# Second stream's low-rank intermediates in their own buffers, and four kinds of scratch stores issued from GpSimd's queue

## The chip, the cores and the metric

The kernel runs on one core of a Trainium2 chip. The engines are TensorE (PE in the profile, with its weight loads listed as PEld), VectorE (DVE), ScalarE (ACT), GpSimd (POOL) and SyncE (SP). SP computes nothing here: its queue issues most of the DMA transfers; GpSimd's queue issues others. Each engine works through its own instructions in order and waits on semaphores for the others. The metric is the device time of one execution in microseconds (us), the median of several runs.

## The reference

A two-layer encoder is applied to two independent requests (here: stream 0 and stream 1), each 512 tokens by 1024 features, in float32, with shared weights.

```python
def _trunk(x, pre_norm_g, post_norm_g, rwkv_params, na_params):
    for i in range(DEPTH):                       # DEPTH = 2
        xn = _rms_norm(x, pre_norm_g[i])
        h = _rwkv7_branch(xn, ...) if i == 0 else _natten_branch(xn, ...)
        x = x + _rms_norm(h, post_norm_g[i])
    return x
# in _rwkv7_branch; lerp(j) = xn + (0.5 * (x_prev + x_next) - xn) * mu[j]
r, k, v, z = lerp(0) @ w_r, lerp(1) @ w_k, lerp(2) @ w_v, xn @ w_z
for d in range(2):                               # forward and backward
    w_log = -softplus(-(w0[d] + tanh(lerp(3 + d) @ w1[d]) @ w2[d])) - 0.5
    decay = exp(-exp(w_log))
    a = sigmoid(a0[d] + (lerp(5 + d) @ a1[d]) @ a2[d])
    y += scan(r, decay, k * (1 + (a - 1) * k_a), v, -kk, kk * a)  # kk: k, scaled and normalised
out = (group_norm(y) + bonus) * silu(z) @ w_o
```

The part that the change touches first is the low-rank pair `tanh(x @ w1) @ w2` and `(x @ a1) @ a2`: 1024 features go down to 64 and up again to 1024, for each of the two directions. The 64-wide intermediates are four arrays per stream (q = 0 to 3). The second layer is a gated attention over a neighbourhood in a 8 by 64 grid.

## The kernel before, in words

Feature rows lie on the 128 partitions and the 512 tokens along the free dimension, so a 1024-feature array is eight tiles of 128x512. Every large product is done as three float32r products of high and low halves (`halves`, L379 and L380; in the scan L743 and L745), accumulated in PSUM.

The program has three stages.

**The prelude** (`prelude`, first for stream 0, then for stream 1) normalises the input, makes the token-shifted mixtures and computes the low-rank intermediates. For each pair of them (`q2` = 0, 1) it forms a 128x512 sum `y` in a buffer `lr` (L582 to L589), and ScalarE writes each 64-row half of it through Tanh or a copy to `u` (L591). `u` is the other half of the same buffer `lr`, so both halves of a pair use one place, and there is one `lr` in all. For stream 0, `u` goes straight to `hidden`, which splits it for later use. For stream 1 it is stored to scratch in HBM (`save("hid", ...)`, L595, which issues in L327) and loaded again when stream 1's turn in the scan comes (L863). Two more buffers of the prelude matter below: `lm`, a 128x514 array with its two edge columns set to zero by GpSimd (L576, L577), and `ls`, four rotating 128x512 buffers that the mixtures pass through on their way to HBM.

**The scan** (`scan_phase`) runs the recurrence in chunks of 64 tokens, 64 steps in all, for both streams. Its instructions are ordered for TensorE, VectorE and ScalarE by a planner (`weave` with the class `Clock`): threads emit steps, and a model of each engine's time chooses which thread goes next. Threads beside the recurrence are: `preps`, which turns k, r and the low-rank arrays into the scan's operands (`prep`: loads `rb` and `k`, then L876; `w2` is split by L878 and L880; L894 and L895 multiply the split weight by the intermediates); `inverse`; `finish`, which normalises a finished output and stores it as `y` (L1316); and `flow`, which feeds big matrix products (L824 to L826) into TensorE's free time, among them the output projection of stream 0, whose result `h` is stored (L1336), and the residual sum `x1` (L781, stored in L782). Where nothing is ready, the planner puts in short idle-filling matmuls (L1641). SP's and GpSimd's own orders follow from the order in which the program emits and from the scheduler's estimates.

**The rest** (`rest`) does the second layer's attention and projections for both streams, with products in L430 to L432.

Scratch loads are always issued from SP (`load`, L333). Scratch stores go through `save` (L325 to L327), whose queue `store` chooses: before the scan SP; from the scan's beginning (`away` is set) GpSimd, except for the kinds `y`, `x1` and `h`, which stay on SP. A store or load waits in its queue until its source is written, or its destination is free, and everything behind it in that queue waits as well.

Names in the profile are those of the program: a DMA `dhid<-lr` is the store of a low-rank intermediate, `dy<-sz` of `y`, `dh<-tmp` of `h`, `dx<-xr` and `dx<-act` of `x1`; `raw` are weights on their way to `whi` and `wlo`.

Of the kernel before, what the change touches and what calls it, by code (L numbers as in the profile page):

```python
# [11 lines left out]
F32 = mybir.dt.float32  # L12
# [7 lines left out]
P = 128  # L20
T = 512
# [210 lines left out]
class Trunk:  # L232
# [94 lines left out]
        self.store(kind).dma_start(d, src)  # L327

    def store(self, kind):
        return self.nc.gpsimd if self.away and kind not in ("y", "x1", "h") else self.nc.sync  # L330

    def load(self, dst, src):
        self.nc.sync.dma_start(dst, src)  # L333
# [168 lines left out]
    def prelude(self, s):  # L502
        nc = self.nc
        vt, gps, act = nc.vector, nc.gpsimd, nc.scalar
        xs = []
        if s == 0:
            self.vectors()
        for k in range(KT):
            if s == 0 and k == self.WFIRST:
                self.first = [self.weight(self.a["w_z"][0])]  # L510
            t = self.t("xn", (P, T + 2), 16, F32, self.lp)
            self.load(t[:, 1:T + 1], self.a["x"][s][k * P:(k + 1) * P, :])
            xs.append(t)
            if s == 0:

                lo, hi = self.pair()
                act.activation(hi, t[:, 1:T + 1], AF.Identity, scale=self.vec("pre0", k))
                vt.scalar_tensor_tensor(lo, t[:, 1:T + 1], self.vec("pre0", k), hi.bitcast(F32), op0=ALU.mult, op1=ALU.subtract)
                self.xz.append((hi, lo))
                yield  # L520
        if s == 0:
            self.consts()
        acc = self.t("acc") if s else self.t("vs", bufs=self.NVS)
        for k, t in enumerate(xs):
            gps.memset(t[:, 0:1], 0.0)
            gps.memset(t[:, T + 1:T + 2], 0.0)
            self.sumsq(acc, t[:, 1:T + 1], k, vt if s or k % 2 else vt)
            yield
        rstd = self.rstd(acc)
        if s == 0:  # L530
            self.rstd0 = rstd
        yield
        xn, xx = [], []
        for k, t in enumerate(xs):
            x = t[:, 1:T + 1]
            vt.scalar_tensor_tensor(x, x, self.vec("pre0", k), rstd, op0=ALU.mult, op1=ALU.mult)
            xn.append(x)
            yield
        if s == 0:
            yield from self.lora_weights()  # L540
        for k, t in enumerate(xs):
            u = self.t("xx", (P, T), 16, F32, self.lp)
            vt.tensor_tensor(u, t[:, 2:T + 2], t[:, 0:T], op=ALU.add)
            xx.append(u)
            yield
        self.shift[s] = xn, xx

        def mixed(kind, j, k):

            t = self.t("ls", (P, T), 4, F32, self.lp)  # L550
            self.lerp(t, xn[k], xx[k], 8 * j + k)
            self.save("l" + kind, s, k, t)

        pm = self.p("pf", (P, 2, T))
        ps = (self.p("pm"), self.p("us"))
        for k in range(KT):
            if s == 0:
                hi, lo = self.xz[k]
            else:
                hi, lo = (self.t("ls", (P, T), 4, F32R, self.lp) for _ in range(2))  # L560
                self.halves(xn[k], lo, hi, self.alt(k))
            for q2 in range(2):
                for out, w in ((pm[:, q2], self.wm), (ps[q2], self.wl)):
                    a, b = (m[:, k % 4] for m in w[2 * q2 + k // 4])
                    nc.tensor.matmul(out, a, hi, start=(k == 0), stop=False)
                    nc.tensor.matmul(out, a, lo, start=False, stop=False)
                    nc.tensor.matmul(out, b, hi, start=False, stop=(k == KT - 1))
                yield
            for kind, j in (("k", 1), ("r", 0), ("v", 2)) if s else ():
                mixed(kind, j, k)  # L570
                yield
        for q2 in range(2):
            mw = self.t("lm", (P, KT * P), 1, F32, self.lp)[:, 0:T + 2]
            lr = self.t("lr", (P, KT * P), 1, F32, self.lp)
            y, u = lr[:, 0:T], lr[0:64, T:2 * T]
            gps.memset(mw[:, 0:1], 0.0)  # L576
            gps.memset(mw[:, T + 1:T + 2], 0.0)  # L577
            if s == 0:
                vt.tensor_tensor(mw[:, 1:T + 1], pm[:, q2], rstd, op=ALU.mult)
            else:  # L580
                act.copy(mw[:, 1:T + 1], pm[:, q2])
            vt.tensor_tensor(y, mw[:, 2:T + 2], mw[:, 0:T], op=ALU.add)  # L582
            yield
            vt.scalar_tensor_tensor(mw[:, 1:T + 1], y, 0.5, mw[:, 1:T + 1], op0=ALU.mult, op1=ALU.subtract)
            if s == 0:
                vt.tensor_tensor(y, ps[q2], rstd, op=ALU.mult)
                vt.tensor_tensor(y, y, mw[:, 1:T + 1], op=ALU.add)
            else:
                vt.tensor_tensor(y, ps[q2], mw[:, 1:T + 1], op=ALU.add)  # L589
            for q in (2 * q2, 2 * q2 + 1):  # L590
                act.activation(u, y[64 * (q % 2):64 * (q % 2) + 64], AF.Tanh if q < 2 else AF.Copy)  # L591
                if s == 0:
                    self.hidden(q, u)
                else:
                    self.save("hid", s, q, u)  # L595
            yield
        if s == 0:
            for k in range(KT):
                mixed("v", 2, k)
                yield  # L600
        if s == 1:
            for k in range(KT):
                self.save("lz", s, k, xn[k])
# [1326 lines left out]
```

## Time and profile before

| | us |
|---|---|
| median of 3 runs (lowest, highest) | 1659.32 (1658.92, 1660.64) |
| the profiled execution's own time | 1659.26 |
| its span, first to last instruction | 1657.5 |
| TensorE busy in it | 1557.6 (94%) |
| VectorE busy | 1217.3 (73%) |
| ScalarE busy | 1013.8 (61%) |
| GpSimd busy | 175.8 (11%) |
| mean granted TensorE clock | 0.975 of full speed |

The profiled execution's time is its span and 1.8 us around it, and it stands at the median of the runs. Times in the text are counted from the start of the span. In the order of time the prelude ends at about 185 us, the scan at about 1165 us. In a timeline row the columns are start, duration, engine, line, operation, `out<-in` with partitions by elements, the count of merged instructions, and in brackets how long the engine stood idle just before and what ended that. Busy time does not count the issuing of DMAs.

### The profile page before, as it was taken

To read this page: it belongs to the slowest core of one execution; us is meant where nothing else is said; L and a number is where in the kernel's file an instruction comes from. 1 tells how busy PE (TensorE), PEld (TensorE's weight loads), DVE (VectorE), ACT (ScalarE), POOL (GpSimd) and SP (SyncE) were. 2 spreads that over 40 slices of the span, in tenths; PEclk is the share of its full clock that TensorE was granted. 3 is DMA by queue.
4 is the path that set the end of the run, shared out by engine and by line. 5 is a ranking of instruction groups with operands and counts; after the bars stand their busy time and mean duration, and the time that the engine had idled before them with its cause. 6 is when DMAs were issued, how large, how long until landed. Compare 5 with 4: busy or idle time off the path is not lost.

```text
span 1657.5 us, 46539 instructions
## 1 busy us (share of the span) xinstructions
PE 1557.6 (94%) x18826; PEld 1197.0 (72%) x18826; DVE 1217.3 (73%) x2711; ACT 1013.8 (61%) x2027; POOL 175.8 (11%) x334
## 2 busy tenths in 40 slices
PE   7989798898999998998988999999999999999998
PEld 6867566776667776776666777777777788777776
DVE  8886469688789787897788897855577585665564
ACT  6567565766755677665575665454567665455562
POOL 0000113311101223010000011000000002100000
PEclk9989899999999999999987999999999999999999
DMA  6455578676687687675776675553765346745553
GB/s 212 154 177 180 163 247 282 211 248 214 228 263 238 209 264 249 207 252 171 243 233 227 201 251 168 178 188 126 265 224 174 109 140 205 246 158 175 171 164 103
DMA packets 176312, 336.29 MB, mean 203 GB/s; under 512 B 20928, under 2 KB 53824, under 8 KB 176096
## 3 DMA queue, kind: packets, MB, share of 16 engines
q1 hardware_dynamic: 152800, 253.60, 48.0%
q0 software_dynamic: 23296, 79.71, 13.6%
q8 instruction: 148, 2.42, 0.6%
q14 instruction: 68, 0.56, 0.1%
HBM read 227.71 MB, written 105.51 MB: 201 GB/s over the span
## 4 chain that ended last, share of the span: by engine, by line
PE 47%; DVE 8%; ACT 5%; DMA 4%; issue 3%; SPq 0%; POOL 0%; DVEq 0%; ACTq 0%; POOLq 0%
PE pg L430 6%; PE pg L431 6%; PE pg L432 6%; PE pm L824 4%; PE pm L825 3%; PE pm L826 3%; PE pf L1112 2%; PE sc L1450 2%; PE po L1483 2%; PE pt L1468 2%; PE us L1231 1%; PE zy L1184 1%; PE us L1211 1%; PE zy L1235 1%; DMA raw<-in_w_in_dram 1%
## 5 line engine op out<-in xcount | busy, mean ns | idle before, releaser
L824 PE MATMUL pm<-act,whi 128*128 128x512 f32 x640 | 285.0, 445 | 8.1 <-ACT act L793 3.2
L825 PE MATMUL pm<-act,whi 128*128 128x512 f32 x640 | 258.0, 403 | 11.7 <-DVE act L771 6.5
L826 PE MATMUL pm<-act,wlo 128*128 128x512 f32 x640 | 256.4, 401 | 5.3 <-DVE wlo L745 5.3
L824 PEld LDWEIGHTS pm<-act,whi 128*128 128x128 f32 x640 | 122.8, 192 | 51.1 <-issue 10.8
L430 PE MATMUL pg<-act,whi 128*128 128x512 f32 x384 | 158.6, 413 | 0.4 <-DVE tmp L1406 0.4
L379 ACT CAST whi<-raw 128x512 fp32r<-128x512 f32 x148 | 91.3, 617 | 106.5 <-PE pg L431 68.7
L431 PE MATMUL pg<-act,whi 128*128 128x512 f32 x384 | 152.6, 397 | 0.0
L432 PE MATMUL pg<-act,wlo 128*128 128x512 f32 x384 | 152.6, 397 | 0.0
L825 PEld LDWEIGHTS pm<-act,whi 128*128 128x128 f32 x640 | 123.5, 193 | 37.9 <-DVE act L771 16.8
L826 PEld LDWEIGHTS pm<-act,wlo 128*128 128x128 f32 x640 | 123.2, 192 | 35.0 <-DVE wlo L745 8.2
L380 DVE TENSOR_TENSOR wlo<-raw,whi 128x512 fp32r<-128x512 f32 x148 | 101.4, 687 | 60.9 <-ACT whi L379 60.2
L745 DVE TENSOR_TENSOR wlo<-raw,whi 128x512 fp32r<-128x512 f32 x160 | 109.1, 684 | 36.4 <-ACT whi L743 36.2
L743 ACT CAST whi<-raw 128x512 fp32r<-128x512 f32 x160 | 97.8, 617 | 42.0 <-PE pm L825 24.3
L430 PEld LDWEIGHTS pg<-act,whi 128*128 128x128 f32 x384 | 72.3, 188 | 15.6 <-issue 3.3
L432 PEld LDWEIGHTS pg<-act,wlo 128*128 128x128 f32 x384 | 72.2, 188 | 14.8 <-issue 0.3
L431 PEld LDWEIGHTS pg<-act,whi 128*128 128x128 f32 x384 | 72.5, 189 | 14.0 <-issue 2.5
L1016 DVE TENSOR_TENSOR etmp<-N 128x30 f32<-128x30 f32 (+14 forms) x240 | 78.6, 328 | 4.3
L1018 DVE TENSOR_TENSOR N<-etmp,N 128x30 f32<-128x30 f32 (+14 forms) x240 | 78.7, 328 | 4.0
L1461 DVE CUSTOM_DVE_ANT_0 sb<-sc,bias 128x256 f32<-128x256 f32 x128 | 49.2, 419 | 27.7 <-PE pt L1468 21.5
L1464 ACT ACTIVATE sb<-sb,mx 128x256 f32<-128x256 f32 x128 | 64.0, 502 | 6.9 <-DVE mx L1463 6.7
L1112 PE MATMUL pf<-cab 64*64 64x128 f32 (+1 forms) x2048 | 66.8, 267 | 0.5 <-issue 0.5
L1135 DVE TENSOR_TENSOR AK<-zy,cc 128x256 f32<-128x256 f32 x63 | 26.6, 422 | 52.0 <-PE zy L1090 51.9
(407 smaller groups left out, 3680.5 us busy)
## 6 DMA issues: line engine op xcount, KB each, us to landing
dab<-ab POOLq DMA_DIRECT2D x32, 1024.0 KB, 7.1
cab<-dab SPq DMA_DIRECT2D x64, 512.0 KB, 4.6
raw<-in_w_in_dram SPq DMA_DIRECT2D x128, 256.0 KB, 3.0
bias<-in_rpb_dram SPq DMA_DIRECT2D x32, 384.0 KB, 5.2
raw<-in_w_z_dram SPq DMA_DIRECT2D x32, 256.0 KB, 3.2
raw<-in_w_k_dram SPq DMA_DIRECT2D x32, 256.0 KB, 3.7
raw<-in_w_r_dram SPq DMA_DIRECT2D x32, 256.0 KB, 3.6
k<-dk SPq DMA_DIRECT2D x32, 256.0 KB, 3.6
```

The source lines that it names most:

```text
L379: self.nc.scalar.copy(hi, src)
L380: (eng or self.nc.vector).tensor_tensor(lo, src, hi.bitcast(F32), op=ALU.subtract)
L430: nc.tensor.matmul(ps, hi, x[k][0], start=(k == 0), stop=False)
L431: nc.tensor.matmul(ps, hi, x[k][1], start=False, stop=False)
L432: self.mm = nc.tensor.matmul(ps, lo, x[k][0], start=False, stop=(k == KT - 1))
L743: nc.scalar.copy(hi, raw[h])
L745: nc.vector.tensor_tensor(lo, raw.pop(h), hi.bitcast(F32), op=ALU.subtract)
L824: nc.tensor.matmul(ps, hi[:, at], xh, start=(k == 0), stop=False)
L825: nc.tensor.matmul(ps, hi[:, at], xl, start=False, stop=False)
L826: nc.tensor.matmul(ps, lo[:, at], xh, start=False, stop=(k == KT - 1))
L1018: vt.tensor_tensor(N[:, q + 1:, :q], tv, N[:, q + 1:, :q], op=ALU.add)
L1112: end = nc.tensor.matmul(st.f[half(a), h, 0, d, g] if st.last else st.f[half(a), h, :, d, g], ab[half(h), d, g, 2 * e[d] + 1 - a], rt if s ...
```

## The change

Two lines decide it. The store's queue is now GpSimd for `hid` always and for every kind once the scan has begun, so that 4 stores of `hid` before the scan and 16 of `y`, 8 of `h` and 8 of `x1` in it move from SP's queue to GpSimd's. And stream 1's four intermediates are written to buffers of the rotating `ls` set, of which there are four, instead of to the second half of `lr`.

```diff
     def store(self, kind):
-        return self.nc.gpsimd if self.away and kind not in ("y", "x1", "h") else self.nc.sync
+        return self.nc.gpsimd if kind == "hid" or self.away else self.nc.sync
...
             for q in (2 * q2, 2 * q2 + 1):
+                if s:
+                    u = self.t("ls", (P, T), 4, F32, self.lp)[0:64]
                 act.activation(u, y[64 * (q % 2):64 * (q % 2) + 64], AF.Tanh if q < 2 else AF.Copy)
                 if s == 0:
                     self.hidden(q, u)
                 else:
                     self.save("hid", s, q, u)
```

No arithmetic is added or removed. Two lines are inserted, so that line numbers from 591 on are two higher in the changed kernel (L591 becomes L593, L743 becomes L745).

The instruction order of the three engines is the same up to the end of the prelude. There it changes in two queues. This is SP's queue before, where the four stores stand between the loads of the last weights (`raw`), of the low-rank weights (`tmp` from `in_lora`) and of the first `prep` (`rb`, `k`, `r`):

```order
L333 DMA raw_1873<-in_w_r_dram 128x512
L327 DMA dhid_379_1554<-lr_1543 64x512
L333 DMA drn_411_1662<-tmp_1657 128x64
L327 DMA dhid_380_1557<-lr_1543 64x512
L333 DMA tmp_1828<-in_lora_dram 128x512
L333 DMA raw_1900<-in_w_r_dram 128x512
L327 DMA dhid_383_1574<-lr_1563 64x512
L327 DMA dhid_384_1577<-lr_1563 64x512
L333 DMA rb_1822<-drn_411_1662 64x512 x2
L333 DMA k_1820<-dk_234_1008 128x512
```

This is SP's queue at the same place with the change:

```order
L333 DMA raw_1877<-in_w_r_dram 128x512
L333 DMA drn_415_1666<-tmp_1661 128x64
L333 DMA tmp_1832<-in_lora_dram 128x512
L333 DMA raw_1904<-in_w_r_dram 128x512
L333 DMA rb_1826<-drn_415_1666 64x512 x2
L333 DMA k_1824<-dk_234_1008 128x512
```

The loads keep their order and nothing of the intermediates stands between them any more.

On ScalarE the activations that write the intermediates (L591, then L593) stood apart before:

```order
L591 ACTIVATE lr_1543<-lr_1543 64x512
L581 COPY lm_1562<-pf_1051 128x512
L591 ACTIVATE lr_1543<-lr_1543 64x512
L655 COPY tmp_1812<-pm_1768 128x512
L743 CAST whi_1836<-raw_1796 128x512
L591 ACTIVATE lr_1563<-lr_1563 64x512
L655 COPY tmp_1858<-pm_1808 128x512
L591 ACTIVATE lr_1563<-lr_1563 64x512
L1670 COPY cab_441_1732<-cc 64x64 x2
L1670 COPY cab_442_1733<-cc 64x64 x2
L878 CAST w2h_1827<-tmp_1828 128x512
```

With the change the two of a pair follow one another, and the weight cast (`whi`) comes behind all four:

```order
L593 ACTIVATE ls_1553<-lr_1543 64x512
L593 ACTIVATE ls_1557<-lr_1543 64x512
L581 COPY lm_1564<-pf_1051 128x512
L657 COPY tmp_1816<-pm_1772 128x512
L593 ACTIVATE ls_1575<-lr_1565 64x512
L593 ACTIVATE ls_1579<-lr_1565 64x512
L745 CAST whi_1840<-raw_1800 128x512
L1672 COPY cab_445_1736<-cc 64x64 x2
L1672 COPY cab_446_1737<-cc 64x64 x2
L657 COPY tmp_1862<-pm_1812 128x512
L880 CAST w2h_1831<-tmp_1832 128x512
```

On VectorE the split of the same weights (`wlo`) moves behind the three operations that form the second pair's sum. From the first store of `y` on (at 412 us in the profile before), the planner's choices differ, since its model gives the two queues different issue times: on TensorE the same products, steps and attention pieces are interleaved in another order up to the scan's end, with 102 idle-filling matmuls in place of 101. GpSimd's queue around that first store of `y`, with the change, between the edge fills (`e`) and operand stores (`dab`) of `prep`:

```order
L959 DMA dab_843_3627<-ab_4796 128x8x256
L917 MEMSET e_1177_5641 128x8
L327 DMA dy_1064_4955<-sz_4722 128x512
L959 DMA dab_843_3627<-ab_4925 128x8x256
L327 DMA dk_1071_4979<-tmp_4977 128x512
L327 DMA dks_1076_5038<-kp_1036_4824 128x512
L327 DMA dy_1082_5070<-sz_4959 128x512
```

Without the two rows of `dy` this is also the order before.

## The prediction

> **What bounds the kernel now.** I read the page's head first, then its chain of work that ended last.
>
> ```profile
> span 1657.5 us, 46539 instructions
> PE 1557.6 (94%) x18826; PEld 1197.0 (72%) x18826; DVE 1217.3 (73%) x2711; ACT 1013.8 (61%) x2027; POOL 175.8 (11%) x334
> PE 47%; DVE 8%; ACT 5%; DMA 4%; issue 3%; SPq 0%; POOL 0%; DVEq 0%; ACTq 0%; POOLq 0%
> ```
>
> TensorE is busy for 94% of the span and carries most of the chain; the queues themselves (SPq, POOLq) carry nothing measurable. The change alters no arithmetic, so what it can move is TensorE's 99.9 us of idle time (1657.5 - 1557.6) and the time it spends at a lowered clock. The next view is the busy time by stretches that I cut at the places the change touches: the seam between prelude and scan (165 to 200), the scan up to the first store of `y` (200 to 412), from there to the stage that forms `x1` (855 to 915), the scan's end, and the rest. Columns are the stretch, its length, the busy time of PE, PEld, DVE, ACT and POOL, the granted clock, the DMA share and GB/s.
>
> ```profile
> 165.00:200.00 35.00, 26.25 (x101) 19.55 (x100) 16.17 (x27) 19.00 (x34) 5.05 (x8) 0.85 0.48 144
> 200.00:412.00 212.00, 192.53 (x2744) 146.38 (x2743) 165.64 (x318) 142.71 (x287) 47.71 (x79) 0.97 0.75 242
> 412.00:855.00 443.00, 414.48 (x7600) 313.14 (x7598) 358.30 (x695) 291.77 (x573) 65.36 (x107) 0.98 0.71 228
> 855.00:915.00 60.00, 51.41 (x724) 38.44 (x724) 50.28 (x91) 35.40 (x65) 3.75 (x6) 0.78 0.76 250
> 915.00:1170.00 255.00, 247.30 (x4326) 189.90 (x4327) 189.98 (x376) 136.57 (x257) 21.83 (x37) 1.00 0.58 186
> 1170.00:1657.00 487.00, 474.57 (x2718) 374.13 (x2716) 303.55 (x958) 278.38 (x632) 30.33 (x56) 0.99 0.55 178
> ```
>
> The seam stands out: TensorE idles for 8.75 of 35 us there, a quarter of it, and runs at a clock of 0.85. In the rest it idles for only 12.4 of 487 us, so I expect nothing there. The seam's timelines show why. TensorE first:
>
> ```profile
> 181.09 1.46 PE L1641 MATMUL zy<-cc 128*128 128x256 f32 x6
> 186.80 0.80 PE L894 MATMUL pm<-h,w2h 128*128 128x512 f32 x1 [4.26 <-ACT w2h L878]
> 191.91 0.80 PE L895 MATMUL pm<-h,w2l 128*128 128x512 f32 x1 [4.31 <-DVE w2l L880]
> 195.49 0.48 PE L824 MATMUL pm<-act,whi 128*128 128x512 f32 x1
> ```
>
> Nearly the whole idle time is two gaps, 4.26 and 4.31 us, at the first `prep`: the split of the low-rank weights comes late from ScalarE (L878) and then from VectorE (L880). VectorE stands behind its own predecessor:
>
> ```profile
> 177.94 0.69 DVE L745 TENSOR_TENSOR wlo<-raw,whi 128x512 fp32r<-128x512 f32 x1 [5.38 <-ACT whi L743]
> 179.17 0.69 DVE L582 TENSOR_TENSOR lr<-lm 128x512 f32<-128x512 f32 x1 [0.54 <-DMA dhid<-lr]
> 190.50 0.75 DVE L876 SCALAR_TENSOR_TENSOR rb<-k,cv,rb 128x512 f32<-128x512 f32 x1 [8.85 <-DMA k<-dk]
> 191.17 0.68 DVE L880 TENSOR_TENSOR w2l<-tmp,w2h 128x512 fp32r<-128x512 f32 x1
> ```
>
> It stood idle 8.85 us until the load of `k` landed. So the question is why that load is late. SP's queue answers:
>
> ```profile
> 173.72 0.54 SPq L327 DMA_DIRECT2D dhid<-lr  x1
> ...
> 178.66 0.33 SPq L333 DMA_DIRECT2D raw<-in_w_r_dram  x1
> 182.12 3.43 SPq L327 DMA_DIRECT2D dhid<-lr  x2
> 185.66 1.18 SPq L333 DMA_DIRECT2D rb<-drn  x2
> 186.89 0.58 SPq L333 DMA_DIRECT2D k<-dk  x1
> ```
>
> The loads of `rb` and `k` stand behind the last two stores of intermediates, and SP is held by these from 179 until 185.5. The stores wait for ScalarE, which in turn waits for the stores:
>
> ```profile
> 173.06 0.63 ACT L591 ACTIVATE lr<-lr 64x512 f32<-64x512 f32 x1
> 173.59 0.56 ACT L581 COPY lm<-pf 128x512 f32<-128x512 f32 x1
> 176.16 0.63 ACT L591 ACTIVATE lr<-lr 64x512 f32<-64x512 f32 x1 [2.00 <-DMA dhid<-lr]
> 177.29 0.62 ACT L743 CAST whi<-raw 128x512 fp32r<-128x512 f32 x1
> 181.47 0.63 ACT L591 ACTIVATE lr<-lr 64x512 f32<-64x512 f32 x1 [3.56 <-DVE lr L589]
> 184.45 0.63 ACT L591 ACTIVATE lr<-lr 64x512 f32<-64x512 f32 x1 [1.89 <-DMA dhid<-lr]
> 186.13 0.62 ACT L878 CAST w2h<-tmp 128x512 fp32r<-128x512 f32 x1
> ```
>
> One place for two intermediates makes the second activation of a pair wait until the first is stored (2.00 and 1.89 us), and the one buffer `lr` makes the second pair wait as well (L582).
>
> **Part one: own places, and stores off SP.** I rebuild the seam from these rows. The first activation stays at 173.06. Activation to the next operation took 0.53 us (173.06 to 173.59), so the second starts at 173.6 and the `lm` copy at 174.1 instead of 173.59. Its 0.56 us end at 174.7, and L582 follows at 174.8 instead of 179.17: nothing in `lr` waits for a store now. From L582 to the third activation took 2.30 us (179.17 to 181.47): it starts at 177.1, the fourth at 177.6. The weight cast `whi` now stands behind them and starts at 178.2 instead of 177.29, its `wlo` (0.65 later, as 177.94 after 177.29) at 178.85. The `raw` load that reuses this buffer went out 0.72 us after `wlo` began (178.66 after 177.94), so at 179.6. With the two stores gone, `rb` follows 0.4 us later at 180.0, `k` 1.23 us after that (186.89 after 185.66) at 181.2. `k` was there 3.61 us after its issue (190.50 after 186.89), so L876 starts at 184.8 instead of 190.50, and L895, which keeps its distance from it, at 186.2 instead of 191.91. The gain is **5.7 us**.
>
> Other conditions come earlier than that. The later cast holds the second column's products by 0.9 us (178.2 for 177.29), so TensorE's filler matmuls end near 183.4. L878 waits for the copy of that column before it in ScalarE's queue and then ends near 183.3, so L894 runs near 183.4 (before: 186.80) and only one gap, some 2.4 us, is left ahead of L895. Every wait that follows (the next loads, `km`, the split of the next weights) hangs on L876 or on TensorE itself, and TensorE was busy for 192.5 of the next 212 us, so I let the whole shift stand to the end. The bounds: at least the 3.4 us by which L894 comes earlier (186.80 - 183.4), at most 8.6 us, both gaps.
>
> The four `hid` stores cost GpSimd one issue each. Behind them on its queue stand a store of `r` and the clearing of `MT`; that clearing comes earlier now, since nothing that it overwrites is still to be stored, and the first edge fill after it has the whole wait for `k` as cover. Without it L876 would still decide.
>
> **The clock at the seam.** From 191.91 to 195.49 each 128x512 product took about 0.43 us from start to start, twice the later step, so 3.6 us of work could take 1.8 us at full clock. Ahead of L895 there is still a gap of 2.4 us, and these rows show what follows such a gap elsewhere (the second is used again below):
>
> ```profile
> 855.88 0.80 PE L826 MATMUL pm<-act,wlo 128*128 128x512 f32 x1 [2.51 <-DVE wlo L745]
> 885.30 0.79 PE L824 MATMUL pm<-act,whi 128*128 128x512 f32 x1 [2.26 <-ACT act L793]
> ```
>
> After 2.51 and 2.26 us of idling the product took 0.80 and 0.79 us, as after 4.26. So I count no gain from the clock (bounds 0 and 1.8). [...]
>
> **Part two: `y`, `h` and `x1` from GpSimd.** What it takes from SP is 32 issues and their waits, what it gives GpSimd is 32 issues:
>
> ```profile
> SPq L327 <- DVE sz L1315: 21.4, 10, 4.8
> SPq L327 <- ACT tmp L1332: 9.3, 5, 3.0
> SPq L333 <- DMA dx<-xr: 4.7, 4, 2.7
> ...
> PE zy L1090 <- DMA cab<-dab: 1.3, 1, 1.3
> ...
> L327 SPq DMA_DIRECT2D dy<-sz x16: 319/326/437, 412.3 to 1168.5; - x16
> L327 POOL DMA_DIRECT2D dz<-tmp x24: 540/540/573, 667.5 to 1611.9; - x24
> ...
> dz<-tmp POOLq DMA_DIRECT2D x24, 256.0 KB, 2.8
> dks<-kp POOLq DMA_DIRECT2D x16, 256.0 KB, 5.9
> dy<-sz SPq DMA_DIRECT2D x16, 256.0 KB, 3.8
> ```
>
> SP saves 32 x 0.33 = 10.6 us of issuing and some 31 us of waiting for `y` and `h`, during which loads stood behind. GpSimd pays 32 x 0.54 = 17.3 us and has 89% of the span free; what stands behind the stores there (`dab`, the next `e`) becomes ready after them in the order shown. Landing is 2.8 to 5.9 us from GpSimd against 3.8 from SP. Who reads: `y` and `x1` are read much later than they are written, but the next `sz` and the next piece of `h` reuse the buffers that the stores read, so there a late landing counts. On TensorE it hardly shows: in the list of its waits a single one, 1.3 us for a load of `cab`, is put down to a transfer, and the others end on VectorE, ScalarE or its own issue. I take **0 us**. The order of work differs from 412 on, and no row shows the new one; the nearest row for what a lucky or unlucky order is worth is the `x1` stage, where TensorE idles 8.6 of 60 us. I keep -8.6 and +8.6 as bounds.
>
> **Sum.** Against the profiled execution's own 1659.26 us, which is at the median of the runs (1659.32): 1659.3 - 5.7 + 0 = **1653.6 us**. Its own range is 1651 to 1656, from the bounds 3.4 and 8.6.
>
> **Rivals.**
>
> *Slower: the `x1` stage waits for GpSimd's stores.* There the loads of further pieces of `h` wait until the store of an earlier `x1` has left its buffer (the row of 4.7 us, four waits), and the chain load, normalise, product is bare: the gap of 2.26 us at 885.30 ends on L793. If each of the four waits grows by the difference between the slowest and the fastest store of GpSimd, 5.9 - 2.8 = 3.1 us, it costs 12.4 us: 1666.0. It ends slower than before by over 0.2% when each wait grows by more than (5.7 + 3.3) / 4 = 2.3 us. Against it: the usual store from GpSimd lands as soon as one from SP. [...]
>
> *The gain is taken back: same.* The seam comes earlier, but the scan's loads cannot: 242 GB/s and a DMA share of 0.75 from 200 to 412 are the highest of the page's stages but one. If they were the bound, or if the new order lost as much, the time would be 1659. Against: the `raw` loads wait mostly for their buffers, which TensorE's progress frees.
>
> *Faster still: the freed SP queue shortens the `x1` stage.* If half of its 8.6 us of idling goes, 1653.6 - 4.3 = 1649.3. For it: stores of `h`, `y` and `x1` stand between the loads there. Against: the gap of 2.51 us at 855.88 ends on a cast that was late in ScalarE's own order.
>
> [...]
>
> **How the numbers follow.** Forecast 0.40, faster still 0.20, full clock 0.06, same 0.17, slower 0.17. Two runs of this kernel differ by up to 0.1%, so about 0.2% (3.3 us, the bound 1656.0 to 1662.6) is what a measurement can tell from no change. Faster is then 0.40 + 0.20 + 0.06 = 0.66, same 0.17, slower 0.17. The range leaves out a tenth on each side: from 1646 (the forecast less most of the 8.6) to 1664 (into the slower case).
>
> **What would show it.** In the changed kernel's seam: no wait of ScalarE on `dhid`, all four activations done by 179, `k` issued near 181, L895 near 186 with at most one gap over 2 us ahead of it, and the idle time between 165 and 195 down to about 3 us. Every later event up to the first `y` shifted by 5 to 6 us. In the `x1` stage: waits of SP for `dx` no longer than before. I am wrong if the shift is there at 200 and gone at 400, if the stretch after the first `y` loses or gains more than 6 us of TensorE's idle or half-clock time, or if `dab` or `e` on GpSimd wait behind a store of `y`.

## The result, and the profile after

The changed kernel takes 1673.68 us (median of 5 runs, 1668.54 to 1676.99) where the kernel before, measured beside it, takes 1660.07 (5 runs, 1658.92 to 1660.73). The ratio is 1.0087, with a 95% interval of 1.0065 to 1.0109: slower by 0.9%, some 14 us, where I had forecast 6 us faster. The profiled execution took 1676.0 us.

The head of its page, and the share of the engines in the chain that ended last:

```profile
span 1674.2 us, 46576 instructions
PE 1559.9 (93%) x18828; PEld 1198.4 (72%) x18828; DVE 1220.7 (73%) x2711; ACT 1012.7 (60%) x2025; POOL 195.1 (12%) x370
PE 69%; DVE 10%; ACT 9%; DMA 7%; issue 5%; POOL 1%; SPq 0%; DVEq 0%; ACTq 0%; POOLq 0%
```

TensorE is busy for 2.3 us more than before (1559.9 against 1557.6) and idle for 114.3 us (1674.2 - 1559.9) where it was 99.9. These 2.3 + 14.4 us are the 16.7 us by which the span grew. GpSimd is busy for 19.3 us longer, which is 36 issues at 0.54 us (on GpSimd's own rows the profile does count the issuing of DMAs as busy), and still for 12%.

The seam, for which the forecast was made, came out as forecast. TensorE's gaps there in the changed kernel, and SP's loads (line numbers are two higher than before, L895 is L897):

```profile
178.82 0.50 PE L826 MATMUL pm<-act,whi 128*128 128x512 f32 x1 [1.03 <-ACT whi L745]
186.50 0.79 PE L897 MATMUL pm<-h,w2l 128*128 128x512 f32 x1 [2.53 <-DVE w2l L882]
```

```profile
179.95 1.31 SPq L333 DMA_DIRECT2D rb<-drn  x2
181.32 0.58 SPq L333 DMA_DIRECT2D k<-dk  x1
```

The load of `k` goes out at 181.32 instead of 186.89, and L895's product starts at 186.50 instead of 191.91. So the loss is elsewhere. These are the changed kernel's busy times by stretches, in the columns that the prediction explained:

```profile
165.00:200.00 35.00, 31.37 (x185) 23.47 (x184) 22.37 (x32) 23.80 (x45) 8.70 (x14) 0.95 0.60 186
200.00:412.00 212.00, 193.41 (x2681) 145.73 (x2687) 165.02 (x318) 139.04 (x280) 47.35 (x79) 0.94 0.72 238
412.00:855.00 443.00, 408.48 (x7573) 308.11 (x7572) 355.87 (x695) 289.11 (x572) 72.47 (x121) 0.98 0.69 226
855.00:1020.00 165.00, 145.91 (x2062) 114.70 (x2061) 140.14 (x262) 96.57 (x178) 21.57 (x38) 0.95 0.70 231
1130.00:1674.00 544.00, 521.91 (x3434) 409.93 (x3425) 330.61 (x1003) 296.90 (x667) 33.02 (x61) 0.98 0.52 170
```

and those of the kernel before for the two stretches that are cut anew:

```profile
855.00:1020.00 165.00, 151.14 (x2199) 115.89 (x2200) 140.98 (x267) 99.37 (x185) 16.66 (x28) 0.92 0.69 228
1130.00:1657.00 527.00, 514.57 (x3173) 405.41 (x3172) 327.86 (x998) 296.29 (x662) 32.49 (x60) 0.99 0.54 175
```

Length less busy time is TensorE's idle time. It falls by 5.1 us at the seam (8.75 to 3.63) and then rises by 6.0 us from 412 to 855 (28.5 to 34.5), by 5.2 from 855 to 1020 (13.9 to 19.1) and by 9.7 from 1130 to the end (12.4 to 22.1). The last is one event, at the scan's end. TensorE there in the changed kernel, the last product and the first scores (`sc`) of the attention:

```profile
1189.00 0.40 PE L432 MATMUL pg<-act,wlo 128*128 128x512 f32 x1
1200.55 2.08 PE L1452 MATMUL sc<-k,q 64*128 64x256 f32 x8 [11.15 <-DMA k<-dk]
```

and in the kernel before:

```profile
1179.67 0.39 PE L430 MATMUL pg<-act,whi 128*128 128x512 f32 x1
1179.99 1.13 PE L1450 MATMUL sc<-k,q 64*128 64x256 f32 x8
```

The changed kernel stands still for 11.15 us until the attention's first `k` has landed, and the scores then take 2.08 us instead of 1.13. The clock follows: in the 24 us from the last product on it is 0.64 (first row, after), where the same place before has 0.93 (second row):

```profile
1189.00:1213.00 24.00, 12.17 (x69) 8.54 (x68) 10.11 (x47) 8.68 (x24) 0.54 (x1) 0.64 0.84 297
```

```profile
1180.00:1204.00 24.00, 20.92 (x138) 15.51 (x138) 16.61 (x79) 16.02 (x43) 0.54 (x1) 0.93 0.81 295
```

SP's queue shows what that `k` stands behind in the changed kernel:

```profile
1187.47 0.33 SPq L333 DMA_DIRECT2D bv<-dv  x1
1191.18 0.33 SPq L333 DMA_DIRECT2D sz<-dz  x1
...
1193.30 0.43 SPq L333 DMA_DIRECT2D q<-dq  x1
1193.77 0.43 SPq L333 DMA_DIRECT2D k<-dk  x1
```

SP waits there from 1187.8 to 1191.2 for the buffer of `sz`, which GpSimd's store of `y` still reads. At first sight this is what the slower rival feared, late stores from GpSimd, though it looked for them in the `x1` stage. But the kernel before issued its `k` no earlier in relation to the last normalisation: 8.9 us after the last transposes of `finish` (L1310, 1163.8 to 1172.7), where the changed kernel takes 6.8 (1187.0 to 1193.8). It had products to do in the meantime. In the order of TensorE's instructions 65 rows of L430 to L432 stand between these transposes and the first scores before, and 4 in the changed kernel.

### The profile page after: what moved, and what is told of

The parts are those of the page before. It is cut to its first block, busy times and chain, and to the rows that moved or that the text cites. A ratio compares the mean times of both kernels' runs of the same rounds, so it can differ in the third digit from the quotient of the medians.

```text
span 1674.2 us, 46576 instructions
## 1 busy us (share of the span) xinstructions
PE 1559.9 (93%) x18828; PEld 1198.4 (72%) x18828; DVE 1220.7 (73%) x2711; ACT 1012.7 (60%) x2025; POOL 195.1 (12%) x370
## 4 chain that ended last, share of the span: by engine, by line
PE 69%; DVE 10%; ACT 9%; DMA 7%; issue 5%; POOL 1%; SPq 0%; DVEq 0%; ACTq 0%; POOLq 0%
PE pm L826 7%; PE pg L430 6%; PE pg L431 6%; PE pg L432 6%; PE pm L827 5%; PE pm L828 5%; DMA dab<-ab 3%; PE pf L1114 2%; PE sc L1452 2%; PE po L1485 2%; PE zy L1186 2%; PE pt L1470 2%; PE us L1233 2%; PE us L1213 2%; PE zy L432 2%
## 5 line engine op out<-in xcount | busy, mean ns | idle before, releaser
L430 PE MATMUL pg<-act,whi 128*128 128x512 f32 x384 | 158.2, 412 | 0.4 <-DVE tmp L1408 0.4
L432 PE MATMUL pg<-act,wlo 128*128 128x512 f32 x384 | 152.3, 397 | 0.0
L745 ACT CAST whi<-raw 128x512 fp32r<-128x512 f32 x160 | 98.0, 619 | 65.5 <-PE pm L827 35.5
L430 PEld LDWEIGHTS pg<-act,whi 128*128 128x128 f32 x384 | 72.2, 188 | 15.8 <-issue 3.3
L432 PEld LDWEIGHTS pg<-act,wlo 128*128 128x128 f32 x384 | 72.2, 188 | 14.9 <-issue 0.3
L1020 DVE TENSOR_TENSOR N<-etmp,N 128x30 f32<-128x30 f32 (+14 forms) x240 | 78.4, 327 | 4.0
L1018 DVE TENSOR_TENSOR etmp<-N 128x30 f32<-128x30 f32 (+14 forms) x240 | 78.2, 326 | 3.8
L1225 ACT COPY X<-us 64x256 f32<-64x256 f32 x128 | 46.8, 366 | 35.8 <-PE zy L1092 32.0
L1114 PE MATMUL pf<-cab 64*64 64x128 f32 (+1 forms) x2048 | 66.5, 265 | 2.1 <-issue 2.0
```

What stands on the lines that cost most here:

```text
L430: nc.tensor.matmul(ps, hi, x[k][0], start=(k == 0), stop=False)
L432: self.mm = nc.tensor.matmul(ps, lo, x[k][0], start=False, stop=(k == KT - 1))
L745: nc.scalar.copy(hi, raw[h])
L1020: vt.tensor_tensor(N[:, q + 1:, :q], tv, N[:, q + 1:, :q], op=ALU.add)
L1114: end = nc.tensor.matmul(st.f[half(a), h, 0, d, g] if st.last else st.f[half(a), h, :, d, g], ab[half(h), d, g, 2 * e[d] + 1 - a], rt if s ...
```

## Experiment 1: the queue or the plan

The change does two things at once from the first `y` on: it issues the stores from another queue, and it makes the planner count them otherwise (900 instead of 380 ns for an issue, and GpSimd's time instead of SP's), which gives another order on TensorE, VectorE and ScalarE. Four kernels take the parts and the two effects apart. All give line numbers as in the kernel before.

Part one alone:

```diff
-        return self.nc.gpsimd if self.away and kind not in ("y", "x1", "h") else self.nc.sync
+        return self.nc.gpsimd if kind == "hid" or self.away and kind not in ("y", "x1", "h") else self.nc.sync
...
+                u = self.t("ls", (P, T), 4, F32, self.lp)[0:64] if s else u; act.activation(u, ...)
```

> Part one alone (own places, hid stored by GpSimd; y, h and x1 stay on SP). TensorE's order is then that of the kernel before, with the 22 rows of each of the three products between the scan's last step and the attention's first scores. Theory 'plan' (the loss comes from the new order, which has used these products up by then): 1653 to 1657, the seam's gain of 3.4 to 5.7 kept. Theory 'queue' (the loss comes from y, h and x1 being issued by GpSimd): the same. If a third one holds, that the loss follows from the earlier seam, it is 1665 or more.

Measured: 1654.10 us (10 runs, 1647.42 to 1659.61), ratio 0.9966 (0.9943 to 0.9989). On the mean of its runs, which scatter over 12 us, the seam's gain holds to the end.

Part two alone (`store` returns GpSimd if `self.away`, nothing else changed):

> Part two alone (y, h and x1 stored by GpSimd; hid stays in lr and on SP). The order has only one row of products there. Both 'plan' and 'queue': 1671 to 1680, a loss of 12 to 20 against the kernel before; TensorE waits about 11 us for the attention's first load of k. If the loss needs both parts, it is near 1660.

Measured: 1678.09 us, ratio 1.0109 (1.0086 to 1.0132), with a wait of 11.01 us for `k`.

The changed kernel, but the planner books the stores of `y`, `h` and `x1` as SP's:

```diff
+            e = self.ENG.get(...); e = "S" if e == "G" and type(i).__name__ == "InstDMACopy" and re.match(r"d(y|h|x1)\d", i.outs[0].bass_ap.tensor.name) else e
```

> Both parts, stores of y, h and x1 from GpSimd, but the planner counts them with SP's price and on SP's queue, so that TensorE's order up to the scan's end is that of the kernel before. 'Plan': 1652 to 1658. 'Queue': 1669 or more, the loads of the attention come late and TensorE waits for them.

Measured: 1652.15 us (1649.84 to 1653.27), ratio 0.9959 (0.9943 to 0.9976).

And the reverse, part one with the stores of `y`, `h` and `x1` on SP, booked as GpSimd's (the same line with "G" and "S" exchanged):

> Part one, and y, h and x1 stored by SP, but the planner counts them with GpSimd's price and on its queue, so that TensorE's order up to the scan's end is that of the changed kernel. 'Plan': 1669 to 1678, with a wait of some 10 us for k near 1200. 'Queue': 1653 to 1658.

Measured: 1673.36 us, ratio 1.0094 (1.0068 to 1.0121). TensorE at the scan's end:

```profile
1197.26 2.08 PE L1450 MATMUL sc<-k,q 64*128 64x256 f32 x8 [10.10 <-DMA k<-dk]
```

The crossing is clean. With the stores on GpSimd and the old plan the kernel is as fast as part one alone (0.9959 and 0.9966); with the stores on SP and the new plan it is as slow as the changed kernel (1.0094 and 1.0087). The queue costs nothing that can be measured, to within 0.3%; the plan costs about 20 us (1.0087 - 0.9966 = 1.2%). The slower rival of the prediction is out: here the wait for `k` is there with `y` stored by SP. The waits that this rival counted, SP's for the buffers that `dx` still reads, did grow. Before they were 4.7 us in four waits; these are the changed kernel's, and those with the new queue and the old plan (total us, times, longest):

```profile
SPq L333 <- DMA dx<-xr: 13.1, 5, 3.9
```

```profile
SPq L333 <- DMA dx<-xr: 10.3, 4, 3.8
```

The second kernel has them too and loses nothing by them.

## Experiment 2: which of part one's two edits opens the seam

Places alone (the activation's line, `store` as before), then the queue of `hid` alone (`store`'s line, `u` as before):

> Of part one only the places of their own; hid is stored by SP as before. If the activations' waits for the stores made k late: the gap ahead of L895 shrinks as with both, L895 at 186 to 188. If the stores' standing in SP's queue did: L895 still at 190 or later.

> Of part one only hid stored by GpSimd; the intermediates stay in lr. If the queue made k late: L895 at 186 to 188, although the activations still wait for their stores. If the shared place did: L895 at 190 or later.

TensorE with the places alone, and with the queue alone:

```profile
178.71 0.51 PE L824 MATMUL pm<-act,whi 128*128 128x512 f32 x1 [1.24 <-ACT whi L743]
183.37 0.50 PE L894 MATMUL pm<-h,w2h 128*128 128x512 f32 x1
186.59 0.51 PE L895 MATMUL pm<-h,w2l 128*128 128x512 f32 x1 [2.73 <-DVE w2l L880]
```

```profile
188.84 0.80 PE L894 MATMUL pm<-h,w2h 128*128 128x512 f32 x1 [6.28 <-ACT w2h L878]
189.57 0.80 PE L895 MATMUL pm<-h,w2l 128*128 128x512 f32 x1
```

The places do it: L895 at 186.59, as with both edits, although the four stores still stand ahead of `k` on SP, since they no longer wait there. The queue alone lets `k` out at 180.30, but ScalarE still waits for its stores (2.32 and 3.61 us ahead of L591), and TensorE waits 6.28 us for the cast `w2h` behind the last of them; L895 comes at 189.57, which lies between what the two readings gave and is 2.3 us earlier than before (191.91). Each kernel ran once, in 1655.91 and 1659.20 us. Both times lie within what the kernel before took beside them (13 runs, 1651.87 to 1665.15), so that only the traces tell the two apart.

## Experiment 3: which stores bring the plan about

> Part one, and of part two only h and x1 (16 stores) from GpSimd; y stays on SP. The planner's order has 4 rows of products ahead of the attention's first scores, as the changed kernel. 'Cover' (what costs is that these products are used up, whichever stores brought the order about): 1669 to 1678, with a wait of about 11 us for k. If y's stores are what costs: 1652 to 1658.

> Part one, and of part two only y (16 stores) from GpSimd; h and x1 stay on SP. The planner's order differs from that of the kernel before from the first y on, but keeps 69 products ahead of the first scores. 'Cover': 1651 to 1658, no wait for k over 1 us. If the different order as such costs, or y's stores: 1665 or more.

In the first, `store` gives GpSimd for `kind == "hid" or self.away and kind != "y"`, in the second for `kind == "hid" or self.away and kind not in ("x1", "h")`.

Measured: `h` and `x1` only, 1667.94 us, ratio 1.0049 (1.0030 to 1.0068), with a wait of 10.60 us for `k`: near what 'cover' expected, a little below its range. `y` only, 1660.32 us (10 runs, 1656.26 to 1667.54), ratio 1.0003 (0.9980 to 1.0026), without a wait for `k`: above its range of 1651 to 1658. Against part one alone the first order costs 0.8% (14 us), the second 0.4% (6 us, and by the two intervals anything from next to nothing to 0.7%). That they add up to the 20 us of the changed kernel is no proof that its order is the sum of these two: each setting gives an order of its own. But there is a loss without the wait for `k`, so not all of it need be at the scan's end.

The order that `y` brings loses earlier. Part one alone, then `y` only, in two stretches:

```profile
412.00:855.00 443.00, 414.20 (x7529) 312.23 (x7528) 357.31 (x692) 291.29 (x572) 64.11 (x105) 0.98 0.71 228
855.00:1020.00 165.00, 149.04 (x2266) 114.43 (x2266) 138.66 (x263) 99.69 (x182) 17.01 (x28) 0.95 0.69 225
```

```profile
412.00:855.00 443.00, 405.88 (x7490) 304.75 (x7489) 351.44 (x688) 284.07 (x559) 68.20 (x112) 0.97 0.69 225
855.00:1020.00 165.00, 145.65 (x2104) 110.92 (x2105) 139.58 (x262) 100.38 (x187) 17.13 (x30) 0.94 0.70 227
```

TensorE idles for 37.1 us instead of 28.8 in the first, 19.3 instead of 16.0 in the second. (Both profiled executions are longer than the medians: 1658.16 us against 1654.10, and 1667.54, the longest of the ten, against 1660.32. So the two stretches show where time goes, and not how much of the 6 us.) One wait goes with this order: VectorE's for the buffer `ab`, until its store `dab` has left it. Before, in the changed kernel, and with the new plan but `y` on SP (total us, times, longest):

```profile
DVE ab L938 <- DMA dab<-ab: 8.5, 5, 3.2
```

```profile
DVE ab L940 <- DMA dab<-ab: 17.7, 8, 3.5
```

```profile
DVE ab L938 <- DMA dab<-ab: 16.9, 7, 4.4
```

It doubles with the order, whichever queue stores `y`; so it is not a `dab` held up behind a store of `y`. That it is what costs the 6 us was not tested.

## Experiment 4: is it the missing cover

The obvious reading of the scan's end is that the products which hid the attention's first loads had been used up. Two kernels put more of the later products ahead of the first scores, and leave the changed kernel's order as it is up to there (12 or 24 steps of the next heads' projections, and the first scores behind the last of them):

```diff
+        a = attention(); next(a)
...
+            g = self.inproj(0, self.xa, p); [next(g) for _ in range(24 if p == self.NPA else 0)]; self.hold = self.mm; run(g, (a, self.POST0))
...
+                        if last or (s, p) == (0, 0):
+                            self.behind(one, last or self.hold)
```

> The changed kernel with its order up to the scan's end as it is, but 72 more rows of the later products (of the last heads' projections) put ahead of the first scores, 76 in all. [...] 'Cover': the wait for k falls below 1 us, no stretch of half clock follows, 1654 to 1662. If something else lies behind the loss (the stores' traffic, the recurrence itself), the wait returns later: 1668 or more.

> [...] 'Cover': a wait of 5 to 7 is left and still drops the clock, 1663 to 1670. If cover isn't the cause: 1671 or more, as the changed kernel.

Measured: 1674.92 us with 24 steps (ratio 1.0091, 1.0066 to 1.0115), 1677.70 with 12 (1.0106, 1.0081 to 1.0131). Both miss what 'cover' expected and lie where I had put them if something else is behind the loss. With 12 the wait for `k` is 9.27 us, where 5 to 7 were expected; why it is so long was not found. (Those 5 to 7 us, and that 24 steps would leave no wait, rested on an estimate of mine for the time of a product that no run shows. In the changed kernel's rows ahead of its wait, 1188.53, 1188.77 and 1189.00, a product takes 0.23 us from start to start, which makes 5.5 us for the 24 rows put ahead with 12 steps and 16.6 for the 72 with 24.) With 24 the wait for `k` is gone, as it should be, and no time is gained. A part of it comes back where the products that were drawn forward are missing, in the attention:

```profile
1337.84 1.52 PE L1468 MATMUL pt<-cc,sb 128*128 128x128 f32 x6 [2.28 <-DVE sb L1466]
1340.09 1.98 PE L1483 MATMUL po<-pts,vtok 128*64 128x128 f32 x16 [0.73 <-ACT pts L1471]
```

The clock from 1335 to 1355 is 0.74. This is not the whole account: from 1130 to the end TensorE idles for 17.3 us here instead of 22.1, and the profiled execution, the slowest of its four, came to the recurrence's last step 4.9 us later than the changed kernel (1155.8 against 1150.9), ahead of anything that was edited. What the two runs do show is that products that cover a wait are a stock, and that drawing them forward from another place gains nothing here. What has to be asked is why the changed order had spent more of them before the recurrence was done: by the order 1556 rows of products stand before its last step, and 1502 in the kernel before.

## Experiment 5: the recurrence's pauses

The recurrence runs in eight groups of eight steps, and between two groups it pauses until the next group's operands are ready. One line of each step (L1112, L1114 in the changed kernel) shows the groups. Its rows for the sixth, seventh and eighth group, with the first and last start in us, before:

```profile
L1112 PE MATMUL pf<-cab x256: 212/270/471, 898.8 to 950.2; 64*64 64x128 f32 x112, 64*64 64x64 f32 x16
L1112 PE MATMUL pf<-cab x256: 217/269/321, 1025.6 to 1072.4; 64*64 64x128 f32 x112, 64*64 64x64 f32 x16
L1112 PE MATMUL pf<-cab x224: 217/269/273, 1096.4 to 1137.7; 64*64 64x128 f32 x96, 64*64 64x64 f32 x16
```

and in the changed kernel:

```profile
L1114 PE MATMUL pf<-cab x256: 218/269/418, 898.7 to 947.7; 64*64 64x128 f32 x112, 64*64 64x64 f32 x16
L1114 PE MATMUL pf<-cab x256: 218/269/272, 1033.0 to 1080.4; 64*64 64x128 f32 x112, 64*64 64x64 f32 x16
L1114 PE MATMUL pf<-cab x224: 218/269/272, 1111.5 to 1150.9; 64*64 64x128 f32 x96, 64*64 64x64 f32 x16
```

The recurrence pauses from 950.2 to 1025.6 before (75.4 us) and from 947.7 to 1033.0 after (85.3), then 24.0 against 31.1 us. The two pauses are 17 us longer, and the last step comes 13 us later (1150.9 against 1137.7). Nothing of this shows as idle time of TensorE in the pauses, where it does products meanwhile: in the longer one it idles for 3.1 us before and for 2.7 after. (The 5.2 us more from 855 to 1020 lie ahead of it, beside the sixth group.) What the seventh group waits for is on VectorE: the elimination in `inverse` (L1016 and L1018, 30 pairs of growing and then shrinking size, closed by L1020). Three of its rows before, and the same three after:

```profile
912.54 0.25 DVE L1018 TENSOR_TENSOR N<-etmp,N 128x84 f32<-128x84 f32 x1
924.59 0.27 DVE L1016 TENSOR_TENSOR etmp<-N 128x108 f32<-128x108 f32 x1
1003.97 1.22 DVE L1020 TENSOR_TENSOR N<-N,cc 128x1024 f32<-128x1024 f32 x1
```

```profile
910.09 0.23 DVE L1020 TENSOR_TENSOR N<-etmp,N 128x84 f32<-128x84 f32 x1
940.60 0.26 DVE L1018 TENSOR_TENSOR etmp<-N 128x108 f32<-128x108 f32 x1
1012.37 1.22 DVE L1022 TENSOR_TENSOR N<-N,cc 128x1024 f32<-128x1024 f32 x1
```

After the third pair the changed order leaves the elimination standing for 30 us in the `x1` stage, behind the steps, `x1` and `prep`; before it was 12. It closes 8.4 us later, and the next group starts 20.3 to 21.6 us after it has closed, in these two and in the four kernels below. In the planner the elimination's thread has rank 5, behind everything on VectorE but the splits of weights not yet needed. Why another price for a store makes the planner leave it standing was not traced.

To make this happen without any moved store, part one alone with one condition on the thread's start (`did["steps"] >= NCH * (n - 1) + 2 * (n == 6)`):

> Part one alone, y, h and x1 on SP as before, and one condition: the seventh elimination may start only two steps of the recurrence later. By the order the pause holds 11.6 columns instead of 10.2, and before the recurrence's last step stand 1556 rows of products, as in the changed kernel (1502 in the kernel before). 'Elimination': the loss comes without any store being moved, 1666 to 1676, pauses of 84 to 90 and about 30, a wait of some 10 for k. Otherwise 1652 to 1658, as part one alone.

Measured: 1670.78 us, ratio 1.0061 (1.0038 to 1.0084), some 16 us above part one alone (1.0061 - 0.9966). Pauses of 82.5 us, a little below the 84 to 90 expected, and 28.5 us, and

```profile
1193.39 2.08 PE L1450 MATMUL sc<-k,q 64*128 64x256 f32 x8 [10.84 <-DMA k<-dk]
```

A late elimination, with the order that the planner builds after it, is enough for the loss at the scan's end. To undo it in the changed kernel, three kernels raise the thread's rank for the seventh elimination (`Thread(lambda: 2.2 if did["inverse"] == 6 else 5, inverse())`, then 1.4 only while `did["steps"]` is below 47, then below 45):

> The changed kernel with one number: the thread of the seventh elimination (VectorE, L1016 and L1018, in the x1 stage) has rank 2.2 in the planner instead of 5. Stores and prices stay as changed. By the order 7.0 columns of products lie in the recurrence's pause before the seventh group instead of 12.4. Theory 'elimination' (VectorE's queue puts this elimination late in the x1 stage, so the recurrence resumes late, products fill the pause and are missing at the scan's end): the pause falls from 86 to below 70, 1648 to 1660, no wait for k at the scan's end. If the late elimination is not the cause: 1668 or more.

> The changed kernel, where the seventh elimination has rank 1.4 only until the 47th step of the recurrence and 5 after that, so that it comes forward only inside the x1 stage. By the order the two pauses then hold 10.9 and 2.5 columns (12.4 and 3.2 in the changed kernel, 10.2 and 2.5 in the kernel before), and 1502 rows of products stand before the recurrence's last step, as in the kernel before. 'Elimination': no wait for k at the scan's end, pauses of 76 to 80 and about 25, 1652 to 1661. If the changed order loses this time wherever the elimination stands, as the earlier run with rank 2.2 throughout leaves possible: 1665 or more, with new waits between 915 and 1020.

> The same with rank 1.4 only until the 45th step. By the order 11.8 and 2.5 columns in the pauses, 1526 rows before the last step and 144 rows of cover after it (114 in the changed kernel, 151 before). 'Elimination': between the two, pauses near 82 and 25, a wait for k of at most 4, 1657 to 1667. Otherwise 1668 or more.

Measured:

| | pauses, us | wait for `k`, us | TensorE idle 855 to 1020, us | median, us | ratio (interval) |
|---|---|---|---|---|---|
| before | 75.4, 24.0 | 0 | 13.9 | 1660.07 | |
| changed | 85.3, 31.1 | 11.15 | 19.1 | 1673.68 | 1.0087 (1.0065 to 1.0109) |
| rank 2.2 | 65.8, 34.2 | 0 | 21.9 | 1667.28 | 1.0046 (1.0028 to 1.0063) |
| 1.4 below 47 | 86.2, 23.9 | 0 | 24.4 | 1665.02 | 1.0033 (1.0013 to 1.0053) |
| 1.4 below 45 | 85.0, 24.1 | 1.85 | 20.8 | 1672.00 | 1.0067 (1.0043 to 1.0092) |

Each does away with the wait for `k`, wholly or nearly, and none comes down to part one alone: all three medians lie above the ranges that I gave for 'elimination', and those of the last two lie where I had put them if the changed order loses this time wherever the elimination stands. The best recovers 9 us of the 20 (1.0087 - 1.0033).

Only rank 2.2 did on the chip what it was meant to do. There the elimination closes 45.5 us after the sixth group's end (994.1 against 948.6), where it took 53.8 before and 64.7 in the changed kernel. With rank 1.4 below step 47 it takes 64.7 again, and below 45 63.7, so that the first pause stays as long:

```profile
1015.98 1.22 DVE L1020 TENSOR_TENSOR N<-N,cc 128x1024 f32<-128x1024 f32 x1
```

What these two change is the order of TensorE's products: with 69 and 58 of them left behind the last transposes the wait for `k` goes, at pauses of 86.2 and 85.0 us. So a long pause alone does not bring the wait about. With rank 2.2 TensorE idles longer between 855 and 1020, where VectorE now owes it the weights' low halves (a wait of 1.60 us for `wlo` at 989.25 and another of 1.54 at 976.40). And none of the three touches what is lost earlier: from 412 to 855 TensorE idles for 34.6, 34.0 and 34.7 us in them, for 34.5 in the changed kernel and for 28.5 before.

So an elimination that stands late in the planner's order brings the wait at the scan's end, as the run with part one alone shows, but it is not the whole of what the changed order loses; the rest is located, and not explained. VectorE's work in that stage is wanted by the recurrence and by the products at once, and with rank 2.2 moving one thread handed the lateness to the other.

## Experiment 6: this order, or any other order

The changed kernel again, with the planner's 900 ns for an issue on GpSimd set to 800 and to 1000. The stores go as in the changed kernel; only the order differs.

> The changed kernel with one number in the planner's model: an issue on GpSimd's queue counts 800 instead of 900. All stores as changed. The order differs from the first store in the scan on from both kernels; it has 12.0 and 1.6 columns in the last two pauses and 155 rows of cover after the recurrence's last step. If only the order of this one price is unlucky: 1651 to 1658. If any order other than that of the kernel before loses (it is the one that the planner's numbers were set for): 1662 or more. By the rows after the last step, no wait for k over 2 in either case.

> The same with 1000. 10.0 and 3.0 columns in the last two pauses, 151 rows of cover. The same two readings: 1651 to 1658, or 1662 or more; no wait for k over 2.

Measured: 1644.83 us with 800 (1641.27 to 1646.95), ratio 0.9904 (0.9874 to 0.9935); 1672.13 us with 1000 (1668.11 to 1678.22), ratio 1.0085 (1.0056 to 1.0113). Neither reading was right: the one order is better than any kernel before it, and the other loses as much as the changed kernel does, at other places. Its pauses are 75.7 and 26.5 us and it never waits for `k`; it loses in the scan. TensorE from 200 to 412 with 800, and with 1000:

```profile
200.00:412.00 212.00, 194.59 (x2690) 146.51 (x2689) 167.33 (x321) 141.40 (x284) 48.55 (x80) 0.98 0.75 243
```

```profile
200.00:412.00 212.00, 187.66 (x2590) 142.33 (x2591) 159.43 (x307) 132.69 (x268) 46.39 (x77) 0.96 0.72 231
```

Between them lie 6.9 us in this stretch alone. With 800 the pauses are 82.1 and 21.7 us, no shorter in sum than before, 69 products are left behind the last transposes, and VectorE waits for `dab` only 4.4 us in all. The orders for 800, 900 and 1000 differ by up to 29 us in their medians, with no trend. The kernel with 800 is faster than both kernels of this change.

## Why the prediction was wrong

The seam was right. `k` at 181.2 was 181.32, L895 at 186.2 was 186.50, the one gap of some 2.4 us was 2.53, the activations ended at 178.1 (by 179), and L895 came 5.4 us earlier where 5.7 were counted. Part one alone, measured to the end, gained 0.34% (0.11 to 0.57), which is 5.6 us with bounds of 2 and 9. One part of the reasoning behind it was too simple: I said that `k` stood behind the stores on SP. It did, but the stores stood there only because of the shared place, and taking that away alone (186.59) does all; taking the queue away alone leaves ScalarE waiting and gains 2.3 us.

No gain from the clock was right too: the product after the gap of 2.53 us took 0.79 us, at a granted clock of 0.51 from 186.2 to 189.6. The 1.8 us that I kept as the upper bound were an estimate from the step of 0.43 us against the later one (0.23 us, 200.10 to 200.34 before), and this run gave none of them. With the places alone the product after 2.73 us of idling took 0.51; see the last section.

That the whole shift stands to the end holds for part one alone in the mean of its runs, and no trace shows it whole. A product at 404.30 before (L1300) comes at 399.94 in the profiled execution of part one alone, 4.4 us earlier, and that execution's span, 1656.4, is only 1.1 us shorter; at 1658.16 us it is one of the slower of its ten. In the changed kernel the product comes at 400.91, 3.4 us earlier. I also took two runs to differ by up to 0.1%, from three: the runs of the kernel before beside the experiments lie between 1651.87 and 1670.23 us, so that a gain of 6 us can be seen only in the mean of several.

The step that failed is part two's "I take 0 us", with its bounds of 8.6 on either side. For the queue the 0 was right: new queue and old plan give 0.9959 against 0.9966. For the order it was not. I wrote that the order differs from 412 on and that no row shows the new one, and then priced it by the idle time of one stage. It cost 20 us, more than twice the bound; the order that `h` and `x1` bring costs 14 by itself, that of `y` 6. The sentence "In the rest it idles for only 12.4 of 487 us, so I expect nothing there" fell with it: from 1130 on there are 9.7 us more of idle time, and the clock is 0.64 from 1189 to 1213 besides. Little idle time says that a stretch is covered, not by how much. What would have told more is the recurrence: it stood still for 75 us under TensorE's products, ended on VectorE's elimination, and had 65 rows of products left behind its last normalisation. In the changed order 54 more products (1556 - 1502) stood ahead of the recurrence's last step, under pauses that were 17 us longer, and 4 rows were left behind that normalisation.

The slower rival gave 1666 and so came nearer to the time, but its mechanism was not the one: the wait for a store from GpSimd is there on SP at 1187.8, and with the stores on SP and the same plan the loss is the same. "The gain is taken back", with "if the new order lost as much", named what happened and sized it at less than a third. Of my own marks, the shift was not gone at 400, no store of `y` held up `dab`, the stretches after the first `y` did lose more than 6 us, and SP's waits for `dx` did get longer (Experiment 1), which cost nothing.

## What to carry to other kernels

Where a planner sets the order, an edit that changes its inputs is two edits: measure them crossed, the new work with the old order and the old work with the new order, before explaining either. An engine that is busy for 97% of a stretch, as TensorE was in the long pause, can be hiding a chain that is late; look for the chain's own pauses (first and last start of one line per group) and for how much covering work is left where it ends. A tuned order is a point among others: three prices 100 ns apart gave 1645, 1674 and 1672 us, so a handful of such numbers is worth trying after any change to the program.

## What the runs showed of the hardware

The length of TensorE's gap ahead of L895 did not tell what clock followed it. In the changed kernel a gap of 2.53 us was followed by a product of 0.79 us, at a granted clock of 0.51 from 186.2 to 189.6; with part one alone the clock of that stretch was 0.51 too. With the places alone the gap was longer, 2.73 us, and the product behind it took 0.51 us, at a granted clock of 1.00. From 183 to 186.2 TensorE was busy for 0.91, 1.06 and 0.79 of the 3.20 us in these three, so that this does not tell them apart either. What sets the clock was not shown.

The 32 stores of `y`, `h` and `x1`, of 256 KB each, cost the same from GpSimd's queue as from SP's in this kernel, within the 0.3% that the two intervals leave open: 0.9959 against 0.9966 with the old plan, 1.0087 against 1.0094 with the new one. An issue took 0.54 us on GpSimd and 0.33 on SP, and no run shows that the kernel's time pays for it.
